# Placing eight gate projections between the last attention heads' scores, with separate buffers for those heads' second exponentials

## The chip, the cores and the metric

The kernel runs on one core of a Trainium2 chip. The metric is device time in microseconds (us) from the start to the end of one execution; the kernel before has a median of 1245.56 us over three runs (1245.56, 1245.99 and 1245.56). The engines are named as the profile names them: PE is TensorE (matrix products), PEld its weight loads, DVE is VectorE, ACT is ScalarE, POOL is GpSimd, SP is the engine that issues most DMAs.

## The reference

A decoder trunk of two layers over 512 tokens with 1024 features, all in float32. Layer 0 mixes with a causal convolution module, layer 1 with differential attention; behind each stand a SwiGLU feed-forward network and a gated per-layer input. The change lies in layer 1, in the attention and in one part of the gated input that is computed early:

```
# differential attention, 8 heads, for each head and each block of 128 queries
logits = q @ k.T + bias          # two components c = 0, 1 of 64 features each
logits = where(dist >= 0, logits, -inf)
probs  = softmax(logits)
w      = probs[c=0] - lam * probs[c=1]
o      = w @ v                    # 128 features per head
o      = rms_norm(o, sub_g) * (1 - lambda_init)
h      = h + concat(o) @ w_o
# ... feed-forward network ...
gate   = sigmoid(rms_norm(h, ple_norm_g) @ ple_w_gate)
h      = h + gate * (p[1] @ ple_w_proj)     # p[1] @ ple_w_proj needs nothing of h
```

## The kernel before, in words

The residual is kept transposed, as eight tiles `h0` to `h7` of 128 features by 512 tokens. A float32 product is made of three float32r matmuls, `mm3` (lines 165 to 169): each operand is split into a high and a low part, and low x high, high x high and high x low are accumulated in PSUM. "A product" below is one such group of three matmuls with 512 columns.

PSUM has four tiles for product sums and the heads' outputs (tag `mm`), two for scores (`sc`) and two for transposes (`tp`), lines 110 to 112.

The attention takes heads in pairs (heads 6 and 7 are pair 3). While the PE makes the projections to queries, keys and values (loop over `QKV`, lines 1291 to 1323), the heads that are ready run between the products as small stages:

- `stage_s(hd, qb)`, lines 1175 to 1208: the scores of one query block, for the components c = 0 and 1. Each is two matmuls (L1195, L1196) with n = 128, 256, 384 or 512 columns, for the block qb = 0 to 3. With n up to 256 both components share one `sc` tile, otherwise each takes its own. DVE then adds the bias and takes the extreme of each row (L1198), reading the `sc` tile and writing a buffer `e`; ACT makes the exponential in place in `e` (L1202); DVE makes the weights from both components (L1205 to L1207). For c = 0 the buffer comes from five rotating tiles, `big`. For c = 1 it is one of two single tiles: `acc` for even blocks, `rb` for odd ones, whatever the head (line 1197).
- `stage_t`, lines 1210 to 1218: up to four transposes on PE into a `tp` tile (L1215), and a copy by ACT to `wth` or `wtl` (L1217).
- `stage_a`, lines 1223 to 1251: the product with the values (L1228) into the head's `mm` tile; after blocks 1 and 3 DVE copies it to SBUF (L1236); after block 3 ACT squares the head's output (L1246) and POOL normalises it (L1247, L1248, L1251).
- `stage_o`, lines 1255 to 1261: four transposes of the head's output (L1258) and its split into high and low parts (ACT L205, DVE L206), which makes input k = hd of the output projection.
- `unit_end`, lines 1146 to 1168: the transposes (L1149) that make queries and keys of 128 tokens from a projection that ACT and POOL (L1143) have normalised, and their scaling and splits (ACT L1157 and L1158, POOL L1162, DVE L1165 and L1167).

The list `stages` (lines 1268 to 1272) holds all stages in order: for each step the scores of one block, `stage_a` of the block four before it and `stage_t` of the block two before it. The last blocks of heads 6 and 7 stand at the end of the order of blocks (lines 1265 to 1267).

27 of these stages are left when the last projection to queries and keys ends. They are run by `step()` (lines 1329 to 1339), which takes the next one from the list, and calls `stage_o` of a head when it is due. Steps are called from the loop over the eight gate projections, `p[1] @ ple_w_proj` (lines 1341 to 1346): each of these is two products (`project`, lines 369 to 376), so there are sixteen products, numbered P1 to P16 here. P1 to P8 take their weights from the tiles `B6` and `B7`, P9 to P16 from tiles that lie in `h0` to `h3`, whose residual was put aside in DRAM and is loaded back after them (`back`, lines 1285 to 1288). There is one step ahead of each projection and one after each product, 24 in all. The rest of the steps is called from the output projection (`linear`, lines 714 to 745, called at line 1364), whose first two output chunks m = 0 and 1 run together over k = 0 to 7.

Within these lists the order on each engine is set by a planner (`schedule_with_timeline_sim=True`, line 1508): the order in which the kernel is written gives the priority, and where an instruction is not yet ready by the planner's own clock, a later one that is ready goes first. Each engine then runs its own list strictly in that order. `tc.issue_after(x)` makes the instructions of a block come behind `x` on `x`'s engine; it is an order, not a wait.

Of the kernel before, what the change touches and what calls it, by code (L numbers as in the profile page):

```python
# [13 lines left out]
F32R = mybir.dt.float32r  # L14
# [6 lines left out]
P = 128  # L21
S = 512
D = 1024
NC = D // P
NH = 8
# [53 lines left out]
LA = 4  # L79
# [1 line left out]
OPS_AT = (1, 2, 4, 5)  # L81
HOOKS = {5: (None,), 6: (1, 3), 7: (0, 2, 4, 5)}
HT = S // 2
E1 = True
GLO = 1
QKV = (("q", 0, (0, 0, 0, 0)), ("v", 0, (1, 1, 1, 2)), ("q", 1, (1, 1, 1, 2)), ("q", 2, (1, 1, 2, 1)), ("v", 1, (1, 1, 2, 2)), ("q", 3, (1, 1, 1, 1)))

# [4 lines left out]
def trunk(ctx, tc, xT, xtok, pT, wts, diag, dww, vec, rel, onehot, lamv, out):  # L92
    nc = tc.nc
    V, A, G, T = nc.vector, nc.scalar, nc.gpsimd, nc.tensor
# [7 lines left out]
    def sb(shape, tag, bufs, dt=F32):  # L102
        uid[0] += 1
        return pool.tile(shape, dt, tag=tag, name=f"{tag}_{uid[0]}", bufs=bufs)
# [9 lines left out]
    big = lambda dt=F32, shape=(P, S): sb(list(shape), "big", 5, dt)  # L114
    f = lambda ap: ap.bitcast(F32)
# [6 lines left out]
    def col(name, i=0):  # L122
        a, _ = VEC[name]
        return vt[:, a + i : a + i + 1]

    ident = sb([P, P], "ident", 1)
# [7 lines left out]
    t = wk()[:, 0:P]  # L134
# [5 lines left out]
    t = tp()  # L140
# [7 lines left out]
    def weight(n=1024, pieces=1, between=(), eng=V, after=(None, None), home=None, parts=None, bufs=1):  # L148
        i = wnext[0]
        wnext[0] += 1  # L150
        raw = sb([P, 1024], *(home or ("wraw", 2)))
        hi = sb([P, 1024], *((parts[0], bufs) if parts else ("whi", 4)), F32R)
        lo = sb([P, 1024], *((parts[1], bufs) if parts else ("wlo", 4)), F32R)
        for k in range(pieces):
            cut = slice(k * n // pieces, (k + 1) * n // pieces)
            loaded[0] = nc.sync.dma_start(raw[:, cut], wts[i, :, cut])
            if k < len(between):
                between[k]()
            with tc.issue_after(after[1].ins) if after[1] else nullcontext():
                A.copy(hi[:, cut], raw[:, cut])  # L160
            with tc.issue_after(after[0].ins) if after[0] else nullcontext():
                eng.tensor_tensor(lo[:, cut], raw[:, cut], f(hi[:, cut]), ALU.subtract)  # L162
        return hi, lo

    def mm3(acc, a, b, first, last, **kw):
        (ah, al), (bh, bl) = a, b
        T.matmul(acc, al, bh, start=first, stop=False, **kw)  # L167
        T.matmul(acc, ah, bh, start=False, stop=False, **kw)  # L168
        return T.matmul(acc, ah, bl, start=False, stop=last, **kw)  # L169
# [15 lines left out]
    def wpart(w, k):  # L185
        return tuple(
            t[k // 4][:, (k % 4) * P : (k % 4 + 1) * P] if isinstance(t, list) else t[:, k * P : (k + 1) * P] for t in w
        )

    def both(t):  # L190
        return t[:, 0], t[:, 1]
# [97 lines left out]
    first = [tuple(sb([P, 1024], t, 4, F32R) for t in ("whi", "wlo")) for _ in range(4)]  # L289
# [69 lines left out]
    def pfeatures(layer, parts):  # L359
        for k, (hi, lo) in enumerate(parts):  # L360
            raw = sb([P, 1024], "wraw", 2)[:, :S]
            nc.sync.dma_start(raw, pT[layer, :, k * S : (k + 1) * S])
            A.copy(hi, raw)
            (G if layer == 0 else V).tensor_tensor(lo, raw, f(hi), ALU.subtract)
        return parts

    last_product = [None]

    def project(ph, m, w, o, step=lambda: None):

        acc = mm()
        for k in range(2):
            last_product[0] = mm3(acc, wpart(w, 2 * (m % 4) + k), ph[k], k == 0, k == 1)
            step()
        last_copy[0] = A.copy(o, acc)
        return o
# [11 lines left out]
    rb = None  # L388
# [161 lines left out]
    for c in range(NC):  # L550
        wa, wg = pairs[c]
        if c == 0:
# [6 lines left out]
            with tc.manual_schedule(engines={T.engine}):  # L559
# [5 lines left out]
                for k in range(NC):  # L565
                    late_rest(a1, pairs[1][0], k)
                    if k == 0:
                        rb = norm.rows()
# [4 lines left out]
        if c == 1:  # L573
            ph = pfeatures(0, [(sb([P, S], t, 2, F32R), sb([P, S], t, 2, F32R)) for t in ("wth", "wtl")])
# [36 lines left out]
    pp = []  # L611
    pw = [weight(), weight()]
# [450 lines left out]
    for k in range(2):  # L1063
        t = tp()
# [5 lines left out]
    def bias(hd):  # L1070
        b = sb([P, S], "bias", 2)
        nc.scalar.dma_start(b, bass.AP(scr.tensor, scr.offset + hd * RW, [[1, P], [1, S]]))
        return b
# [72 lines left out]
    def unit_end(pair, tb, q):  # L1146
        t = tp()
        for i in range(4):
            T.transpose(t[:, i * P : (i + 1) * P], q[:, i * P : (i + 1) * P], ident)  # L1149
        t4 = t.rearrange("p (h c t) -> p h c t", h=2, c=2)  # L1150
        cut = slice(tb * P, (tb + 1) * P)
        qs, ks, kl = qk[pair][0:2], qk[pair][2:4], qk[pair][4:6]

        qg, kg = col("q_g"), gains[:, 0:1]
        for c in range(2):
            own, other = HALVES[c], HALVES[1 - c]
            A.activation(qs[c][own, :, cut], t4[own, :, 0], AF.Copy, scale=qg[own])  # L1157
            A.activation(ks[c][own, :, cut], t4[own, :, 1], AF.Copy, scale=kg[own])  # L1158
            if KDUP == "A":
                A.activation(ks[c][other, :, cut], t4[own, :, 1], AF.Copy, scale=kg[own])  # L1160
            else:
                G.tensor_copy(ks[c][other, :, cut], f(ks[c][own, :, cut]))  # L1162
        for c in range(2):
            own, other = HALVES[c], HALVES[1 - c]
            V.scalar_tensor_tensor(  # L1165
                qs[c][other, :, cut], t4[own, :, 0], qg[own], f(qs[c][own, :, cut]), ALU.mult, ALU.subtract)
            V.scalar_tensor_tensor(  # L1167
                kl[c][own, :, cut], t4[own, :, 1], kg[own], f(ks[c][own, :, cut]), ALU.mult, ALU.subtract)

    last_block = [None, None]  # L1170
    biases = {}
    stats = {}
    state = {}

    def stage_s(hd, qb):
        if qb == 0:
            biases[hd] = bias(hd)
        b = biases[hd]
        n = (qb + 1) * P
        brev = bass.AP(b.tensor, b.offset + (S - 1) - (S - n), [list(b.ap[0]), [-1, n]])  # L1180
        qs, ks, kl = qk[hd // 2][0:2], qk[hd // 2][2:4], qk[hd // 2][4:6]
        i = hd % 2
        if qb == 0:
            stats[hd] = sb([P, 4, 6], "st", 2)
        es, st = [], stats[hd][:, qb]
        for c in range(2):
            cut = slice(qb * P, (qb + 1) * P)
            if not PACK or n > S // 2:
                acc = sc()
            elif c == 0:  # L1190
                both = sc()
                acc = both[:, : S // 2]
            else:
                acc = both[:, S // 2 :]
            T.matmul(acc[:, :n], qs[c][:, i, cut], ks[c][:, i, 0:n], start=True, stop=False)  # L1195
            T.matmul(acc[:, :n], qs[c][:, i, cut], kl[c][:, i, 0:n], start=False, stop=True)  # L1196
            e = sb([P, S], ("acc", "rb")[qb % 2], 1) if c and E1 else big()
            V.tensor_tensor_reduce(  # L1198
                out=e[:, :n], in0=acc[:, :n], in1=brev, scale=-1.0, scalar=3.0e38,
                op0=ALU.add, op1=ALU.min, accum_out=st[:, c : c + 1],  # L1200
            )
            A.activation(e[:, :n], e[:, :n], AF.Exp, scale=-1.0, bias=st[:, c : c + 1], accum_out=st[:, 2 + c : 3 + c])  # L1202
            es.append(e)

        V.reciprocal(st[:, 4:5], st[:, 3:4])  # L1205
        V.scalar_tensor_tensor(st[:, 5:6], st[:, 4:5], mlam, st[:, 2:3], ALU.mult, ALU.mult)
        last_block[0] = V.scalar_tensor_tensor(es[0][:, :n], es[1][:, :n], st[:, 5:6], es[0][:, :n], ALU.mult, ALU.add)  # L1207
        state[hd, qb] = es[0]
# [46 lines left out]
    def stage_o(hd):  # L1255
        t = tp()
        for i in range(4):
            T.transpose(t[:, i * P : (i + 1) * P], osb[hd][:, i * P : (i + 1) * P], ident)  # L1258
        hi, lo = both(sb([P, 2, S], f"A{hd}", 1, F32R))
        split_scaled(t, gains[:, 1:2], hi, lo)  # L1260
        ot[hd] = (hi, lo)
# [3 lines left out]
    todo = [(hd, qb) for hd in range(NH) for qb in range(4)]  # L1265
    todo.append(todo.pop(todo.index((NH - 2, 3))))
    todo.append(todo.pop(todo.index((NH - 1, 3))))
    stages = []
# [22 lines left out]
    for what, at, pace in QKV:  # L1291
        ws = slab(GLO if at > 0 else 0)
        for tb in range(4):
# [10 lines left out]
            if (what, at, tb) == ("q", 0, 1):  # L1304
                ph = pfeatures(1, [both(sb([P, 2, S], t, 1, F32R)) for t in ("B4", "B5")])
            elif (what, at, tb) == ("q", 0, 2):
                n = wnext[0]
                wnext[0] = PROJ1
                pw = [weight(parts=("B6", "B7"))]
# [17 lines left out]
    done, steps = [0], [0]  # L1327

    def step():

        steps[0] += 1
        if stages:
            n, s = stages.pop(0)
            s()
        else:
            n = 99
        while done[0] < NH and n >= todo.index((done[0], 3)) + LA + 4 and steps[0] > 4 * done[0] + 3:
            stage_o(done[0])
            done[0] += 1

    pp = []
    for m in range(NC):
        if m % 2 == 0:
            o2 = sb([P, 2, S], f"C{m // 2 + 2}", 2)
        step()
        pp.append(project(ph, m, pw[m // 4], o2[:, m % 2], step))

    def heads_until(k):
        while done[0] <= k:
# [13 lines left out]
    order = {m: last_block for m in (2, 3, 4, 5)}  # L1363
# [149 lines left out]
```

## Time and profile before

| | |
|---|---|
| median of the runs | 1245.56 us |
| the profiled execution | 1243.71 us |
| its span, first to last instruction | 1241.9 us |
| PE busy | 1230.2 us, 7048 matmuls |
| DVE, ACT, POOL busy | 878.7, 624.8, 464.9 us |
| the attention's scores L1195 | 627.4 to 790.9 us |
| the sixteen products of the gate projections | 766.9 to 793.7 us |

Times in the trace are us from the start of the span. A line of the timeline gives the start, the duration, the engine, the line of the kernel, the operation, the tile written and those read, the shape, and in brackets how long the engine was idle just before and what ended that. A matmul's duration is a modelled one and overlaps the next; the distance from one start to the next is what it costs. A line of the windows gives, for a stretch, the busy time of each engine with the number of its instructions, then the granted clock of PE (1.00 is full), the busy share of the DMA engines and GB/s.

### The profile page before, as it was taken

What the parts mean: (1) busy time and instruction counts of PE and PEld (TensorE: products, weight loads), DVE (VectorE), ACT (ScalarE), POOL (GpSimd) and SP (SyncE); (2) the same over time, 40 slices, a digit from 0 to 9 for tenths busy, and PEclk for the clock granted to TensorE, in tenths of its full rate; (3) what the DMA queues carried; (4) which work ended last, traced back from release to release, by engine and by line L of the source; (5) the groups of instructions that cost most, each with busy time, mean ns of one, the idle gap of its engine ahead of it and who ended that gap; (6) DMA issues with size and microseconds to landing.
All of it is one profiled execution on the core that took longest, in us unless ns stands there. A gap on an engine that the chain in (4) does not pass through costs nothing.

```text
span 1241.9 us, 18364 instructions
## 1 busy us (share of the span) xinstructions
PE 1230.2 (99%) x7048; PEld 1077.1 (87%) x7048; DVE 878.7 (71%) x1244; ACT 624.8 (50%) x1098; POOL 464.9 (37%) x351
## 2 busy tenths in 40 slices
PE   9999999999999999999999999999999999999998
PEld 7888788888998899888788888788889998999887
DVE  5999765975895479547677876647966885588535
ACT  7743454533553255435566877735434552455432
POOL 0953422024570454142436635041026640562220
PEclk9999999999999999999999999999999999999999
DMA  9655323233333332334432331142233333233331
GB/s 329 227 179 179 93 69 118 89 106 112 101 90 119 100 96 75 102 107 151 139 111 63 109 98 30 52 151 87 89 126 91 103 115 109 83 103 88 104 97 68
DMA packets 50020, 138.44 MB, mean 111 GB/s; under 512 B 5732, under 2 KB 10852, under 8 KB 49933
## 3 DMA queue, kind: packets, MB, share of 16 engines
q1 hardware_dynamic: 47664, 133.71, 34.2%
q10 hardware_dynamic: 2268, 3.57, 1.0%
q8 instruction: 55, 0.90, 0.3%
q14 instruction: 33, 0.26, 0.1%
HBM read 130.94 MB, written 6.31 MB: 111 GB/s over the span
## 4 chain that ended last, share of the span: by engine, by line
PE 84%; DVE 7%; DMA 3%; issue 3%; ACT 2%; POOL 2%; SPq 0%; ACTq 0%; DVEq 0%; POOLq 0%
PE mm L167 26%; PE mm L168 26%; PE mm L169 26%; DVE sc L508 2%; POOL wk L496 2%; DMA wraw<-in_wts 1%; DVE wlo L162 1%; PE mm L1228 1%; DMA B<-po 1%; PE sc L1195 1%; PE sc L1196 1%; PE tp L1215 1%; PE tp L1149 1%; DMA po<-big 0%; DVE wlo L822 0%
## 5 line engine op out<-in xcount | busy, mean ns | idle before, releaser
L160 ACT CAST whi<-wraw 128x1024 fp32r<-128x1024 f32 (+1 forms) x139 | 141.0, 1024 | 220.0 <-PE mm L169 106.8
L162 DVE TENSOR_TENSOR wlo<-wraw,whi 128x1024 fp32r<-128x1024 f32 (+1 forms) x135 | 174.2, 1296 | 82.5 <-ACT whi L160 81.8
L167 PE MATMUL mm<-A,wlo 128*128 128x512 f32 (+1 forms) x546 | 212.1, 388 | 0.1
L168 PE MATMUL mm<-A,whi 128*128 128x512 f32 (+1 forms) x546 | 211.1, 387 | 0.0
L169 PE MATMUL mm<-A,whi 128*128 128x512 f32 (+1 forms) x546 | 208.9, 387 | 0.1
L167 PE MATMUL mm<-B,wlo 128*128 128x512 f32 x352 | 137.0, 389 | 0.0
L168 PE MATMUL mm<-B,whi 128*128 128x512 f32 x352 | 137.0, 389 | 0.0
L169 PE MATMUL mm<-B,whi 128*128 128x512 f32 x352 | 135.6, 389 | 0.0
L228 POOL TENSOR_TENSOR acc<-acc,wk 128x512 f32<-128x512 f32 x35 | 60.3, 1724 | 191.6 <-ACT wk L227 190.9
L168 PE MATMUL mm<-C,whi 128*128 128x256 f32 x448 | 126.8, 283 | 0.0
L169 PE MATMUL mm<-C,whi 128*128 128x256 f32 x448 | 126.8, 283 | 0.0
L167 PE MATMUL mm<-C,wlo 128*128 128x256 f32 x448 | 126.8, 283 | 0.0
L167 PEld LDWEIGHTS mm<-A,wlo 128*128 128x128 f32 x546 | 102.7, 188 | 21.6 <-DVE h L1359 0.5
L169 PEld LDWEIGHTS mm<-A,whi 128*128 128x128 f32 x546 | 102.6, 188 | 21.5 <-DVE A L206 0.8
L168 PEld LDWEIGHTS mm<-A,whi 128*128 128x128 f32 x546 | 102.7, 188 | 20.3
L822 DVE TENSOR_TENSOR wlo<-A,whi 128x1024 fp32r<-128x1024 f32 x60 | 104.9, 1758 | 20.4 <-ACT whi L821 20.4
L821 ACT CAST whi<-A 128x1024 fp32r<-128x1024 f32 x60 | 62.9, 1048 | 55.0 <-PE mm L169 43.9
L831 POOL TENSOR_TENSOR A<-wraw 128x512 f32<-128x512 f32 x16 | 24.0, 1500 | 168.4 <-DMA wraw<-in_wts 143.3
L831 POOL TENSOR_TENSOR A<-A 128x512 f32<-128x512 f32 x16 | 25.1, 1566 | 163.6 <-DMA A<-in_wts 160.9
L167 PEld LDWEIGHTS mm<-C,wlo 128*128 128x128 f32 x448 | 86.0, 192 | 0.2
L168 PEld LDWEIGHTS mm<-C,whi 128*128 128x128 f32 x448 | 86.0, 192 | 0.2
L169 PEld LDWEIGHTS mm<-C,whi 128*128 128x128 f32 x448 | 86.0, 192 | 0.0
(332 smaller groups left out, 3065.3 us busy)
## 6 DMA issues: line engine op xcount, KB each, us to landing
wraw<-in_wts SPq DMA_DIRECT2D x159, 512.0 KB, 3.6
A<-in_wts SPq DMA_DIRECT2D x32, 512.0 KB, 3.6
wraw<-in_wts SPq DMA_DIRECT2D x16, 384.0 KB, 3.1
D<-in_diag SPq DMA_DIRECT2D x22, 256.0 KB, 4.8
C<-in_diag SPq DMA_DIRECT2D x16, 256.0 KB, 5.0
h<-in_xT SPq DMA_DIRECT2D x8, 256.0 KB, 3.9
B<-in_xtok SPq DMA_DIRECT2D x4, 512.0 KB, 7.7
rest<-h SPq DMA_DIRECT2D x8, 256.0 KB, 2.7
```

Source lines behind the costliest of these rows:

```text
L160: A.copy(hi[:, cut], raw[:, cut])
L162: eng.tensor_tensor(lo[:, cut], raw[:, cut], f(hi[:, cut]), ALU.subtract)
L167: T.matmul(acc, al, bh, start=first, stop=False, **kw)
L168: T.matmul(acc, ah, bh, start=False, stop=False, **kw)
L169: return T.matmul(acc, ah, bl, start=False, stop=last, **kw)
L228: self.last = self.eng.tensor_tensor(self.acc, self.acc, sq, ALU.add)
L496: G.tensor_tensor(pacc, pacc, pr, ALU.add)
L508: last_v_tap[0] = V.scalar_tensor_tensor(sum_, tap(j), wt(c, j), sum_, ALU.mult, ALU.add)
L821: A.copy(hi, src)
L822: V.tensor_tensor(lo, src, f(hi), ALU.subtract)
L831: G.tensor_tensor(s[:, 0], r1[:, 0], r1[:, 1], ALU.add)
L1149: T.transpose(t[:, i * P : (i + 1) * P], q[:, i * P : (i + 1) * P], ident)
```

## The change

The change makes three things.

Buffers: the second exponentials (c = 1) of heads 6 and 7 no longer go to `acc` and `rb`. Head 6 gets a tile of two halves under the tag `C0`, head 7 one under `C1`; the half is chosen by the parity of the block. These tags have two slots each; the slot that is taken held the queries of pair 2.

Order of the stages: the first eleven of the 27 left stages come in an order written out by hand.

Pace: a table says which steps follow each product, instead of one step after each. The letter `s` is a step, `S` a step whose PE instructions are put behind the product just made. There is one step ahead of P1, and 18 in the loop, so 19 instead of 24 before the output projection. P7 and P8 come behind the last `unit_end`'s transposes, and each product from P10 on comes behind the last score written so far. `stage_o` falls due a few steps later for heads 0 to 2 (at steps 7, 10 and 13, instead of 4, 8 and 12).

So on PE the written order is: scores (6,1), P1, P2, then P3 to P9, scores (6,2), P10, scores (7,0), P11, scores (7,1), P12, P13, transposes of (6,0), P14, scores (7,2), P15, scores (6,3), P16, scores (7,3), with the other stages between them; (6,2) is head 6, block 2.

```diff
-E1 = True
+PACE1 = ("","s","ss","","","","","","","S","S","Ss","","Sss","sSss","sss","s")
...
-    def project(ph, m, w, o, step=lambda: None):
+    def project(ph, m, w, o, step=lambda: None, gate=nullcontext):
         acc = mm()
         for k in range(2):
-            last_product[0] = mm3(acc, wpart(w, 2 * (m % 4) + k), ph[k], k == 0, k == 1)
+            with gate():
+                last_product[0] = mm3(acc, wpart(w, 2 * (m % 4) + k), ph[k], k == 0, k == 1)
             step()
...
     def unit_end(pair, tb, q):
-            T.transpose(t[:, i * P : (i + 1) * P], q[:, i * P : (i + 1) * P], ident)
+            turned[0] = T.transpose(t[:, i * P : (i + 1) * P], q[:, i * P : (i + 1) * P], ident)
...
     def stage_s(hd, qb):
-            T.matmul(acc[:, :n], qs[c][:, i, cut], ks[c][:, i, 0:n], start=True, stop=False)
+            first = T.matmul(acc[:, :n], qs[c][:, i, cut], ks[c][:, i, 0:n], start=True, stop=False)
+            if c == 0 or n > S // 2:
+                last_score[0] = first
             T.matmul(acc[:, :n], qs[c][:, i, cut], kl[c][:, i, 0:n], start=False, stop=True)
-            e = sb([P, S], ("acc", "rb")[qb % 2], 1) if c and E1 else big()
+            if c and hd >= NH - 2:
+                k = 2 * (hd % 2) + qb % 2
+                if k // 2 not in late_e:
+                    late_e[k // 2] = sb([P, 2, S], f"C{k // 2}", 2, F32R)
+                e = f(late_e[k // 2])[:, k % 2]
+            elif c:
+                e = sb([P, S], ("acc", "rb")[qb % 2], 1)
+            else:
+                e = big()
...
-        while done[0] < NH and n >= todo.index((done[0], 3)) + LA + 4 and steps[0] > 4 * done[0] + 3:
+        while done[0] < NH and n >= todo.index((done[0], 3)) + LA + 4 and steps[0] > max(4 * done[0] + 3, 3 * done[0] + 6):
...
+    order = [(stage_s, 6, 1), (stage_a, 5, 1), (stage_t, 5, 3), (stage_a, 5, 2), (stage_s, 6, 2),
+             (stage_s, 7, 0), (stage_s, 7, 1), (stage_a, 5, 3), (stage_t, 6, 0), (stage_a, 6, 0), (stage_t, 6, 1)]
+    rank = {at: i for i, at in enumerate(order)}
+    stages.sort(key=lambda s: rank.get((s[1].func, *s[1].args), len(order)))
+    products = [0]
+
+    def spaced():
+        products[0] += 1
+        for kind in PACE1[products[0]]:
+            with tc.issue_after(last_product[0].ins) if kind == "S" else nullcontext():
+                step()
+
+    def gate():
+        return tc.issue_after(last_score[0].ins) if products[0] > 8 else nullcontext()
+
+    step()
     for m in range(NC):
         if m % 2 == 0:
             o2 = sb([P, 2, S], f"C{m // 2 + 2}", 2)
-        step()
-        pp.append(project(ph, m, pw[m // 4], o2[:, m % 2], step))
+        with tc.issue_after(turned[0].ins) if m == 3 else nullcontext():
+            pp.append(project(ph, m, pw[m // 4], o2[:, m % 2], spaced, gate))
```

More of the change, by code (lines that the diff above doesn't have):

```diff
@@ L1170, in trunk @@
     last_block = [None, None]
+    late_e = {}
+    turned = [None]
+    last_score = [None]
     biases = {}
```

## The prediction, made before the changed kernel had run

> **What bounds the kernel now.** I read the page first, then the windows around the sixteen products, then the timelines of PEld, PE, DVE, ACT and POOL there.
>
> ```profile
> span 1241.9 us, 18364 instructions
> ...
> PE 1230.2 (99%) x7048; PEld 1077.1 (87%) x7048; DVE 878.7 (71%) x1244; ACT 624.8 (50%) x1098; POOL 464.9 (37%) x351
> ...
> PEclk9999999999999999999999999999999999999999
> ...
> PE 84%; DVE 7%; DMA 3%; issue 3%; ACT 2%; POOL 2%; SPq 0%; ACTq 0%; DVEq 0%; POOLq 0%
> ```
>
> PE is busy 99% of the span at full clock, and 84% of the chain that ended last is PE. So the change can win only time in which PE stands still, and 1241.9 - 1230.2 = 11.7 us of that exist in the whole kernel. The windows say how much lies where the change works:
>
> ```profile
> 766.00:776.00 10.00, 10.00 (x59) 8.47 (x58) 5.63 (x18) 7.12 (x20) 4.78 (x7) 1.00 0.01 2
> 776.00:783.00 7.00, 5.11 (x35) 4.16 (x34) 6.61 (x25) 6.66 (x23) 1.64 (x4) 1.00 0.01 2
> 783.00:787.00 4.00, 4.00 (x21) 3.26 (x19) 2.50 (x9) 2.47 (x7) 1.40 (x2) 1.00 0.18 42
> 787.00:792.00 5.00, 5.00 (x35) 4.29 (x34) 4.15 (x12) 4.61 (x16) 0.00 (x0) 1.00 0.20 71
> 792.00:807.00 15.00, 15.00 (x93) 12.97 (x91) 7.33 (x17) 9.30 (x23) 0.00 (x0) 1.00 0.22 71
> 822.00:850.00 28.00, 28.00 (x123) 23.18 (x124) 18.79 (x21) 15.06 (x22) 12.31 (x7) 1.00 0.37 108
> ```
>
> The columns after the length are PE, PEld, DVE, ACT and POOL. Only from 776 to 783 does PE stand (5.11 of 7.00); there DVE (6.61) and ACT (6.66) are nearly full. Right behind, from 783 to 787, it is the other way round: PE is full and DVE and ACT have 1.5 us free each. This is the clump that the change takes apart:
>
> ```profile
> 774.72 0.60 PE L1149 MATMUL tp<-ident,big 128*128 128x128 f32 x4
> ...
> 782.63 0.48 PE L167 MATMUL mm<-B,h 128*128 128x512 f32 x1
> 782.94 0.39 PE L168 MATMUL mm<-B,h 128*128 128x512 f32 x1
> 783.17 0.40 PE L169 MATMUL mm<-B,h 128*128 128x512 f32 x1
> ...
> 786.59 0.39 PE L169 MATMUL mm<-B,h 128*128 128x512 f32 x1
> ...
> 792.09 0.48 PE L167 MATMUL mm<-B,h 128*128 128x512 f32 x1
> ```
>
> P9 to P14 run as eighteen matmuls without a break from 782.63 to 786.59; P15 and P16 start at 792.09. A matmul of 512 columns costs 783.17 - 782.94 = 0.23 us, a product 0.69.
>
> **The waits that are to go.** [...]
>
> ```profile
> 776.44 0.19 PEld L1195 LDWEIGHTS sc<-C,C 128*128 128x128 f32 x1 [0.16 <-DVE st L1198]
> ...
> 777.26 0.19 PEld L1195 LDWEIGHTS sc<-C,C 128*128 128x128 f32 x1 [0.52 <-DVE st L1198]
> ...
> 778.49 0.42 PEld L1258 LDWEIGHTS tp<-ident,D 128*128 128x128 f32 x4 [0.69 <-ACT wtl L1217]
> ...
> 780.14 0.19 PEld L1195 LDWEIGHTS sc<-C,C 128*128 128x128 f32 x1 [0.23 <-DVE st L1198]
> ...
> 781.60 0.19 PEld L1195 LDWEIGHTS sc<-C,C 128*128 128x128 f32 x1 [1.16 <-DVE st L1198]
> ```
>
> The sum is 0.16 + 0.52 + 0.69 + 0.23 + 1.16 = 2.76 us. Four of the five wait for DVE to read a score out of one of the two `sc` tiles, one for ACT's copy out of a `tp` tile.
>
> [...]
>
> **Part by part.**
>
> *Pace and gates.* One product (0.69) now stands by order between each two of the scores (6,2), (7,0), (7,1), (7,2), (6,3), (7,3), two behind (7,1). Six products make 4.1 us of cover where 2.76 us are waited. The first, second and fourth wait (0.16, 0.52, 0.23) are each shorter than a product: gone. The fifth (1.16) is longer than P14 alone, but the buffers shorten it, next part. The third (0.69) belongs to `stage_o` of an early head, which now falls due later, with P12 and P13 near it; ACT must still get through its copies, so this wait may return: bounds 0 and 0.69. I take 0.15 as left over of all five.
>
> *The buffers.* These are the DVE rows that hold the fifth wait:
>
> ```profile
> 773.39 0.48 DVE L1165 SCALAR_TENSOR_TENSOR C<-tp,vec,C 64x256 fp32r<-64x256 f32 x1 [2.73 <-ACT C L1158]
> ...
> 780.25 0.48 DVE L1207 SCALAR_TENSOR_TENSOR big<-rb,st,big 128x256 f32<-128x256 f32 x1
> ...
> 781.12 0.41 DVE L1198 CUSTOM_DVE_ANT_0 rb<-sc,bias 128x256 f32<-128x256 f32 x1
> ...
> 781.46 0.61 DVE L1207 SCALAR_TENSOR_TENSOR big<-acc,st,big 128x384 f32<-128x384 f32 x1
> 781.99 0.74 DVE L206 SCALAR_TENSOR_TENSOR A<-tp,mhalf,A 128x512 fp32r<-128x512 f32 x1
> 782.65 0.28 DVE L1198 CUSTOM_DVE_ANT_0 acc<-sc,bias 128x128 f32<-128x128 f32 x1
> ...
> 787.60 0.56 DVE L1198 CUSTOM_DVE_ANT_0 acc<-sc,bias 128x384 f32<-128x384 f32 x1 [2.06 <-PE sc L1196]
> ```
>
> The second component of (7,1) can go into `rb` at 781.12 only once (6,1) is read out of it (780.25 to 780.73); that of (7,0) waits for (6,2) to leave `acc` (781.46) and is read at 782.65. Each holds an `sc` tile meanwhile. With a tile per head neither pair shares a buffer. This wins what is left of the fifth wait, nothing beyond. Where the later blocks' chain becomes shorter (`rb` is shared by (6,3) and (7,3) too) it costs and wins nothing, because PE is full from 792 to 807 anyway.
>
> *Breaks.* The first long matmul behind short ones costs 782.94 - 782.63 = 0.31 instead of 0.23: its weights, 0.19 in the PEld rows, can't load under a short predecessor. So a product by itself costs 0.08 more. Between 0 and 7 breaks are new (0 to 0.56 us); I take three, 0.25, since products behind scores of 384 and 512 columns, and P13 behind P12, have a long predecessor.
>
> *P7 and P8 behind the last `unit_end`.* It takes two products, 1.38 us, from the cover ahead of the transposes at 774.72. Were these late, PE would stand up to 1.38 us. They are not:
>
> ```profile
> 770.69 1.04 POOL L1143 TENSOR_TENSOR big<-big,r 128x512 f32<-128x512 f32 x1
> ```
>
> ```profile
> 773.01 0.48 PE L167 MATMUL mm<-B,B 128*128 128x512 f32 x1
> ```
>
> The input is ready at 771.73, and PE is in other work until 773.01, where P7 starts now. The edit costs nothing, and the splits behind these transposes start earlier, towards DVE's idle 2.73 us that end at 773.39.
>
> *The end.* P15 and P16 (1.38 us) now run ahead of the last score instead of behind it, and the last eight stages come from the output projection, behind its first products. So the cover of the last chain shrinks. Its rows:
>
> ```profile
> 796.07 0.75 DVE L1207 SCALAR_TENSOR_TENSOR big<-rb,st,big 128x512 f32<-128x512 f32 x1
> ...
> 805.72 2.36 DVE L162 TENSOR_TENSOR wlo<-wraw,whi 128x1024 fp32r<-128x1024 f32 x2 [0.30 <-ACT whi L160]
> ```
>
> ```profile
> 803.46 0.60 PE L1215 MATMUL tp<-ident,big 128*128 128x128 f32 x4
> ...
> 807.09 0.47 PE L167 MATMUL mm<-A,wlo 128*128 128x512 f32 x1
> ...
> 815.81 0.60 PE L1258 MATMUL tp<-ident,D 128*128 128x128 f32 x4
> ```
>
> ```profile
> 811.67 2.07 POOL L1251 TENSOR_TENSOR D<-D,r 128x512 f32<-128x512 f32 x1
> ```
>
> The weights of (7,3) are ready at 796.82 and transposed only at 803.46: 6.6 us of slack, more than 1.38. The head's normalisation ends at 813.74, PE asks for it at 815.81: 2.07 us of slack. If the planner puts the last transposes behind all products that cover them, the 3.63 us from 803.46 to 807.09 (copy, weight split, first product) would lose their two products, 1.38 us. I take 0.
>
> *Queues.* The moved scores of (7,0) issue one DMA, head 7's bias, on ACT's queue:
>
> ```profile
> 760.51 0.33 ACTq L1072 DMA_DIRECT2D bias<-scr  x1
> ```
>
> It goes some 16 us before DVE reads it. The loads of `h0` to `h3` on SP start when P9 to P16 are done; those end no later than before.
>
> **The sum.** 2.76 - 0.15 - 0.25 = 2.36 us. Against the profiled execution: 1243.71 - 2.36 = 1241.35, with a span near 1239.5. The median of the runs lies 1.85 us above that execution; moved by as much, it becomes 1245.56 - 2.36 = 1243.2. With the bounds (waits left 0 to 1.2, which is the second and third; breaks 0 to 0.56) the gain is 1.0 to 2.76, so 1242.8 to 1244.6. A measurement of this kernel tells about 0.2% from no change, 2.5 us, so this forecast lies at that edge.
>
> **The rivals.**
>
> *ACT is the bound of the stretch.* Its work from 776 to 792 is 6.66 + 2.47 + 4.61 = 13.74 us; at the share that it reaches under load, 6.66 / 7.00 = 95%, this takes 14.4 of the 16 us. So no more than 1.6 us could be won before the last scores, 1.3 after the breaks: 1244.3. For it speaks the third wait; against it, that PE can go on with the output projection while ACT catches up.
>
> *More than the idle rows.* With smoother DVE and ACT, some of the dozen breaks that already stand between 776 and 822 (0.08 each) go too, about 1 us: 2.36 + 0.9 = 3.3, 1242.3. Against it: PE takes as many turns between short and long matmuls as before.
>
> *The order turns against PE.* Before, PE's list held any ready product. Now P10 to P16 stand behind scores by order, and if a score waits for DVE, all of them wait. DVE has four splits of early heads (L206, 0.75 each) which the planner can put ahead of the reads that free `sc`. Then 4 x 0.75 = 3.0 us come on top of the 2.76 that stay: 1245.56 + 3.0 = 1248.6. It decides where DVE's work between two scores outlasts the product there, 0.69. For it: DVE is at 6.61 of 7.00 from 776 to 783. Against it: from 783 to 792 DVE works 6.65 of 9.00 and PE never stands.
>
> *The planner places as before.* Its own clock, not the chip, decided the clump; but `S` and the gates are orders it has to keep, so this is unlikely: 1245.6.
>
> **How the numbers follow.** Forecast 0.56, ACT bound 0.14, more than the rows 0.12, order against PE 0.14, no effect 0.04. Faster by over 0.2% needs 2.5 us: 0.24 of the forecast's 0.56 and all of the 0.12, together 0.36. Slower by over 0.2%: 0.10 of the 0.14 of the third. Within: 0.32 + 0.14 + 0.04 + 0.04 = 0.54. The range runs from the second rival's 1242.3, less 0.2, to 1245.9, which takes in the forecast, the ACT bound and no effect and leaves out the slower case: 1242.1 to 1245.9.
>
> **What would show it.** In the profile after, the PEld rows of the scores (6,2) to (7,3) should have no wait above 0.3 us on L1198, matmuls of one product each between them, the second components written to `C` and not to `acc` or `rb`, and DVE's idle 2.06 us at 785.5 gone. PE's busy time should stay near 1230 and the span fall by 2.4. I am wrong if a wait of PE above 0.5 us stands between 774 and 793, or a new one at the first products of m = 2 or at the last heads' L1258 between 800 and 822.

## The result and the profile after

The changed kernel takes 1241.3 us (median of six runs, 1240.72 to 1242.19), the kernel before in the same comparison 1245.57 (six runs, 1244.4 to 1247.1). The ratio is 0.9971, its 95% interval 0.9961 to 0.9981. So the change is faster, by 0.29% (0.19 to 0.39%), and the time lies 0.8 us below the low end of the predicted range.

The page of the changed kernel, whose profiled execution took 1242.19 us, has in its span, its busy times and its chain of work:

```profile
span 1240.4 us, 18361 instructions
...
PE 1229.5 (99%) x7048; PEld 1077.3 (87%) x7048; DVE 879.7 (71%) x1244; ACT 624.5 (50%) x1098; POOL 463.4 (37%) x351
...
PE 88%; DVE 5%; issue 3%; DMA 2%; ACT 1%; POOL 0%; SPq 0%; ACTq 0%; DVEq 0%; POOLq 0%
```

The matmuls are the same 7048, PE's share of the chain rose from 84% to 88%, and DVE's fell from 7% to 5%. The span of these two executions fell by only 1.5 us, less than the 4.27 us between the medians. The windows, in the same stretches as before, say where PE's idle time went:

```profile
766.00:776.00 10.00, 10.00 (x57) 8.62 (x56) 5.63 (x16) 7.78 (x22) 5.74 (x9) 1.00 0.01 2
776.00:783.00 7.00, 7.00 (x43) 6.18 (x42) 6.63 (x23) 6.10 (x19) 1.82 (x3) 1.00 0.11 20
783.00:787.00 4.00, 4.00 (x26) 3.60 (x25) 3.37 (x15) 3.49 (x13) 1.06 (x2) 1.00 0.27 100
787.00:792.00 5.00, 5.00 (x33) 4.35 (x32) 4.58 (x14) 4.62 (x16) 0.00 (x0) 1.00 0.23 67
792.00:807.00 15.00, 15.00 (x94) 12.91 (x93) 8.33 (x15) 9.15 (x26) 2.09 (x3) 1.00 0.26 75
```

From 776 to 783 PE is now full (7.00 for 5.11) and runs 43 matmuls for 35, while DVE is as busy as ever: 6.63 us, before 6.61. DVE was not made faster; PE has other work while it waits for DVE. The weight loads of the scores now have no wait at all, and one wait is left in the whole part from 766 to 806, in PEld:

```profile
804.52 0.19 PEld L167 LDWEIGHTS mm<-A,wlo 128*128 128x128 f32 x1 [0.26 <-PE mm L1242]
```

(The new lines shift the numbers: a score is L1199 and L1202 for L1195 and L1196, DVE's read of it L1212 for L1198, `stage_t` L1229 for L1215, `stage_a` L1242 for L1228, `stage_o` L1272 for L1258.) In PE's timeline P10, P11, P15 and P16 now stand singly among the scores; P12 to P14 run from 780.84 to 783.0, ahead of the second components of (7,0) and (7,1):

```profile
767.56 0.39 PE L167 MATMUL mm<-B,B 128*128 128x512 f32 x1
...
777.60 0.39 PE L167 MATMUL mm<-B,h 128*128 128x512 f32 x1
...
779.14 0.33 PE L1199 MATMUL sc<-C,C 128*128 128x128 f32 x1
...
779.42 0.45 PE L167 MATMUL mm<-B,h 128*128 128x512 f32 x1
...
782.24 0.27 PE L1229 MATMUL tp<-ident,big 128*128 128x128 f32 x1
782.27 0.47 PE L167 MATMUL mm<-B,h 128*128 128x512 f32 x1
782.58 0.39 PE L168 MATMUL mm<-B,h 128*128 128x512 f32 x1
...
800.92 0.60 PE L1229 MATMUL tp<-ident,big 128*128 128x128 f32 x4
...
803.17 1.06 PE L1242 MATMUL mm<-B,wtl 128*128 128x128 f32 x8
803.98 0.48 PE L169 MATMUL mm<-A,B 128*128 128x512 f32 x1
804.55 0.47 PE L167 MATMUL mm<-A,wlo 128*128 128x512 f32 x1
```

The second exponentials go to `C`, and DVE's idle 2.06 us are gone:

```profile
783.42 0.29 DVE L1212 CUSTOM_DVE_ANT_0 C<-sc,bias 128x128 f32<-128x128 f32 x1 [0.32 <-PE sc L1202]
```

**A measure that holds from run to run.** PE's matmuls are the same 4260, in the same order, up to P1, and the same again from the first product of the output chunk m = 2 on (for three kernels further below this second half does not hold). Between these two starts lies all that the change touches; this distance is called the window below. Its two ends after are the rows at 767.56 and 804.55: 36.99 us. Before, P1 starts at

```profile
766.94 0.39 PE L167 MATMUL mm<-B,B 128*128 128x512 f32 x1
```

and m = 2 at 807.09 (shown in the prediction): 40.15 us. The window became 3.16 us shorter. In the profiled execution after, P1 began 0.62 us later and the part behind the window (span less its end) took 1240.4 - 804.55 = 435.85 us, before 1241.9 - 807.09 = 434.81, so 1.04 more, with the same instructions. 3.16 - 0.62 - 1.04 = 1.50 us, which is the fall of the span. Whether the change makes those 1.66 us, or the runs do, is the first question for the experiments.

### The profile page after: what moved, and what is told of

The parts are those of the page before. It is cut to its first block, busy times and chain, and to the rows that moved or that the text cites. A ratio compares the mean times of both kernels' runs of the same rounds, so it can differ in the third digit from the quotient of the medians.

```text
span 1240.4 us, 18361 instructions
## 1 busy us (share of the span) xinstructions
PE 1229.5 (99%) x7048; PEld 1077.3 (87%) x7048; DVE 879.7 (71%) x1244; ACT 624.5 (50%) x1098; POOL 463.4 (37%) x351
## 4 chain that ended last, share of the span: by engine, by line
PE 88%; DVE 5%; issue 3%; DMA 2%; ACT 1%; POOL 0%; SPq 0%; ACTq 0%; DVEq 0%; POOLq 0%
PE mm L167 27%; PE mm L169 26%; PE mm L168 26%; PE sc L458 2%; DVE wlo L823 2%; PE mm L1242 1%; DMA wraw<-in_wts 1%; PE sc L1202 1%; PE sc L1199 1%; PE tp L1229 1%; DVE B L914 1%; PE tp L1150 1%; DMA po<-big 1%; DVE wk L906 0%; DVE sc L509 0%
```

## The experiments

In the tables and texts, "last score" is the start of the second component of (7,3), counted from P1. Before it is 24.0 us, after 24.2.

**Is it the window, or something outside it?** Theory A: the products' placing acts in the window alone and the rest is chance between runs. Theory B: part of the gain (or a loss) lies outside. Theory C: the buffers are what takes the waits away, the products' placing is beside the point. Four kernels ran side by side, then two more on another chip.

`again` and `again2` are the changed kernel, unaltered; `null` is the kernel before, unaltered.

> The changed kernel once more, unaltered, to separate the change from what differs from run to run. In the two traces PE needs 40.15 us from P1 to the first product of m = 2 before and 36.99 after, 3.16 less; the medians differ by 4.3. Theory A (the change acts in this window alone, and the rest is chance in DMA waits elsewhere): the window is again 37.0 +- 0.1, the difference of the medians falls to 3.2 +- 0.7. Theory B (something outside the window is faster as well, such as the loads of h0 to h3 or the output projection's weights): the medians differ by 4 or more again and a stretch outside the window is shorter in this trace as well.

> The changed kernel a third time, on the same chip as the kernel before run as a candidate. Theory A: window 36.99 +- 0.1; median 3.2 +- 0.8 below that of before. Theory B: 4 or more below.

> The kernel before, unaltered, timed against itself, with a profile of its own. Theory A (the window alone changes, the rest of the difference is chance): the window from P1 to the first product of m = 2 is 40.15 +- 0.1 again, the median lies within 1 us of the other runs of before, and the start of P1 and the rest behind the window differ from the first profile by up to 2 us each with identical instructions. Theory B (the change wins outside the window too): P1 starts later or the rest behind the window is longer than in the changed kernel's profiles, 764.7 to 767.6 and 434.8 to 435.9.

| kernel | its median (runs) | kernel before beside it | ratio, 95% interval |
|---|---|---|---|
| again | 1240.09 (5) | 1244.13 (23) | 0.9965, 0.9952 to 0.9977 |
| again2 | 1241.02 (11) | 1243.83 (23) | 0.9976, 0.9967 to 0.9984 |
| null | 1244.53 (12) | 1243.83 (23) | 1.0002, 0.9993 to 1.0011 |

The ends of the window in `again`, `again2` and `null`, from PE's timelines:

```profile
764.72 0.39 PE L167 MATMUL mm<-B,B 128*128 128x512 f32 x1
...
801.70 0.47 PE L167 MATMUL mm<-A,wlo 128*128 128x512 f32 x1
```

```profile
768.22 0.39 PE L167 MATMUL mm<-B,B 128*128 128x512 f32 x1
...
805.19 0.47 PE L167 MATMUL mm<-A,wlo 128*128 128x512 f32 x1
```

```profile
766.00 0.39 PE L167 MATMUL mm<-B,B 128*128 128x512 f32 x1
...
806.12 0.47 PE L167 MATMUL mm<-A,wlo 128*128 128x512 f32 x1
```

The windows are 36.98, 36.97 and 40.12 us: each kernel's window repeats within 0.03 us. Outside it the times scatter: P1 starts at 764.72 and at 768.22 in two executions of one program, and the kernel before starts it at 766.94 and 766.00. `again` by itself met what had been written down for B: 4.04 us between the medians, and P1 2.2 us earlier than before. `again2` and `null` speak against it: 2.81 us between the medians, and P1 of `again2` comes later than in either trace of the kernel before. So A stands and B falls. Over all runs the changed kernel has a median of 1241.13 us (22 runs, 1238.31 to 1242.19), the kernel before 1244.26 (66 runs with those of `null`, 1241.84 to 1247.1); the difference, 3.13, agrees with the window's 3.16.

**Which of the parts does it?** `buffers` is the kernel before with the new buffers alone:

```diff
-            e = sb([P, S], ("acc", "rb")[qb % 2], 1) if c and E1 else big()
+            if c and hd >= NH - 2:
...
+                e = f(late_e[k // 2])[:, k % 2]
```

> The kernel before with the separate buffers for heads 6 and 7 alone; order, pace and gates as before. Theory A (the placing of the products removes the waits, the buffers only shorten the fifth): the clump P9 to P14 stays, the first four waits (1.6 us) stay, of the fifth (1.16) some 0.5 to 1.1 goes; gain 0.5 to 1.1 us. Rival C (the sc tiles held by acc and rb are the cause of the waits, the placing does nothing): waits of the scores on L1198 fall below 0.3 each and the gain is 2 to 3 us.

1244.16 us (11 runs) against 1244.13, ratio 1.0001 (0.9992 to 1.0009); window 39.82 us, 0.33 less than before, so less than the 0.5 to 1.1 that theory A gave it too. The two small waits of 0.17 at the last score, shown further below, are gone. The fifth wait moves on by one score:

```profile
780.30 0.34 PE L1196 MATMUL sc<-C,C 128*128 128x384 f32 x1
...
781.56 0.19 PEld L1196 LDWEIGHTS sc<-C,C 128*128 128x128 f32 x1 [1.06 <-DVE st L1207]
```

```profile
781.08 0.41 DVE L1207 CUSTOM_DVE_ANT_0 C<-sc,bias 128x256 f32<-128x256 f32 x1
```

The first component of (7,2), which waited 1.16 before, runs at 780.30 without a wait: with a buffer of its own (7,0) leaves its `sc` tile earlier. But the second component of (7,2) then waits 1.06 for the other tile. DVE reads (7,1) out of that at 781.08, 14.3 us behind P1 (before, at 781.12, 14.2), without idle time ahead of it: there it is DVE's list that holds the tile, and not a shared buffer.

`pace` is the changed kernel with the old buffers:

```diff
-            if c and hd >= NH - 2:
...
-            else:
-                e = big()
+            e = sb([P, S], ("acc", "rb")[qb % 2], 1) if c else big()
```

> The changed kernel with acc and rb for the second exponentials of heads 6 and 7 again; order, pace and gates stay. Theory A: gain 2 to 2.7 us, with a wait of up to 0.5 us at a score of (7,1) or (7,2). Rival C: the waits come back, gain under 1 us, since P10 to P16 now stand behind scores that acc and rb hold up.

1241.58 us (10 runs), ratio 0.9978 (0.9969 to 0.9987), window 36.96. No wait at a score came back, where up to 0.5 us had been expected. So the buffers bring nothing in the changed kernel, and C falls.

`no_orders` keeps the table but not the orders on PE: a step marked `S` is a plain step, and products no longer come behind the last score.

```diff
-            with tc.issue_after(last_product[0].ins) if kind == "S" else nullcontext():
+            with tc.issue_after(last_product[0].ins) if False else nullcontext():
...
-        return tc.issue_after(last_score[0].ins) if products[0] > 8 else nullcontext()
+        return tc.issue_after(last_score[0].ins) if False else nullcontext()
```

> The changed kernel without the orders S and without the gates from P10 on: list, number of steps, due steps of stage_o, the order behind the last unit_end and the buffers stay. The planner is free again to pull products forward, and in the written order four of them (P9 to P12) go ahead of (6,2) in one clump. Theory A: two or three of the waits come back behind the clump, gain 0.5 to 1.8 us. Rival C (buffers) and rival D (the list of stages and the later stage_o remove the waits, the orders are an ornament): gain 3 us as with the orders.

1241.56 us (8 runs), ratio 0.9974 (0.9963 to 0.9984), window 37.09. P9 to P12 now run in one clump ahead of (6,2), the last score comes only at 27.4 us, and still PEld has a single wait in the window:

```profile
805.65 0.19 PEld L167 LDWEIGHTS mm<-A,wlo 128*128 128x128 f32 x1 [0.26 <-PE mm L1242]
```

This was a surprise: the orders that my prediction built on, one product between each two scores, are not needed either.

**The list, the due steps or the number of steps?** What is left is the order of the stages by hand, the later `stage_o`, and the table's plain numbers: fewer steps ahead of P9 to P16. Theory D: the list, or the later `stage_o`, takes the waits away. Theory E: the pace does, as the last heads' scores then meet products that are still to be made. Two kernels take one part out of the changed kernel (`old_due` has the old condition for `stage_o`, `no_list` lacks the sort), two put one part into the kernel before (`list_only` has the list alone; `bare_pace` the numbers of the table as plain steps, one step ahead of the loop, and nothing else):

```diff
+    PACE1 = ("", "s", "ss", "", "", "", "", "", "", "s", "s", "ss", "", "sss", "ssss", "sss", "s")
...
+    step()
     for m in range(NC):
...
-        step()
-        pp.append(project(ph, m, pw[m // 4], o2[:, m % 2], step))
+        pp.append(project(ph, m, pw[m // 4], o2[:, m % 2], spaced))
```

> The changed kernel, but stage_o of heads 0 to 2 falls due at steps 4, 8 and 12 again. The window from P1 to the first product of m = 2 was 40.15 before and 36.99, 36.99, 36.96 and 37.09 in four kernels with pace and list, so one profile tells. Theory E (it is the pace, fewer steps ahead of P9 to P16, that lets the planner take products where scores are not yet freed): window 37.0 to 37.3. Theory D (the third wait, 0.69, was that of an early stage_o; the list and the later due steps remove the waits): 37.6 to 38.5, with a wait of PE at L1258's counterpart behind ACT.

> The changed kernel without the hand-written order of eleven stages: they come in the list's old order, with the same pace, orders and due steps. Theory E: window 37.0 to 37.3. Theory D: some waits come back, 37.8 to 39.

> The kernel before with nothing but the hand-written order of the eleven stages; 24 steps, one after each product and one ahead of each projection, old due steps and buffers. Theory E: the waits stay, 39.3 to 40.5. Theory D: 37.0 to 38.5.

> The kernel before with nothing but the pace: 19 steps behind the products as in the changed kernel's table, no orders, no list, old due steps, old buffers. Theory E: window 37.0 to 37.5, nearly all of the change's 3.16. Theory D: 38.5 to 40, as the list and the due steps are missing.

| kernel | window, us | last score, us | one run, us (before beside it: 1245.08) |
|---|---|---|---|
| old_due | 37.03 | 26.8 | 1240.22 |
| no_list | 37.01 | 27.4 | 1241.92 |
| list_only | 40.47 | 29.3 | 1244.98 |
| bare_pace | 41.07 | 30.2 | 1246.79 |

D falls: each of its parts can be left out (`pace_orders`, below, has neither), and the list alone wins nothing. Its waits only move; the three longest of seven in PEld are:

```profile
776.08 0.42 PEld L1215 LDWEIGHTS tp<-ident,big 128*128 128x128 f32 x4 [0.90 <-PE sc L1196]
...
777.79 0.42 PEld L1258 LDWEIGHTS tp<-ident,D 128*128 128x128 f32 x4 [0.53 <-ACT wtl L1217]
...
781.67 0.30 PEld L1228 LDWEIGHTS mm<-B,wth 128*128 128x128 f32 x2 [0.76 <-ACT wth L1217]
```

E holds in its first half only. The bare pace removes the waits at the scores (of before's 3.27 us one of 0.48 is left), and yet its window is the longest of all. The loss has another place, as PEld shows:

```profile
783.38 0.42 PEld L1258 LDWEIGHTS tp<-ident,D 128*128 128x128 f32 x4 [0.48 <-ACT wth L1217]
...
804.36 0.97 PEld L1228 LDWEIGHTS mm<-B,wtl 128*128 128x128 f32 x8 [0.66 <-ACT wtl L1217]
...
808.06 0.48 PEld L1258 LDWEIGHTS tp<-ident,D 128*128 128x128 f32 x4 [2.74 <-POOL D L1251]
```

The way there is read in PE's timeline of the same kernel:

```profile
791.73 0.48 PE L167 MATMUL mm<-A,h 128*128 128x512 f32 x1
...
797.77 0.48 PE L1195 MATMUL sc<-C,C 128*128 128x512 f32 x1
...
803.07 0.60 PE L1215 MATMUL tp<-ident,big 128*128 128x128 f32 x4
...
808.07 0.89 PE L1258 MATMUL tp<-ident,D 128*128 128x128 f32 x4 [2.55 <-POOL D L1251]
808.60 0.77 PE L167 MATMUL mm<-A,wlo 128*128 128x512 f32 x1
```

The planner takes products of the output projection (`mm<-A,h`, from 791.73 on) ahead of the last scores, the second component of (7,3) starts only at 797.77, 30.2 us behind P1, and its weights are transposed at 803.07. By then the products of m = 0 and 1, which should cover the chain of the last two heads (copy by ACT, product with the values, normalisation on POOL), are used up: PE waits 0.66 for ACT's copy and 2.74 for the transposes of head 6, which the row puts down to POOL. The sum, 0.48 + 0.66 + 2.74 = 3.88 us, is more than before's 3.27.

POOL is not alone in this. PE's list has head 6's transposes (808.07) ahead of the first product of m = 2 (808.60), while in the kernel before and in every kernel with a window near 37 they stand 6.9 us behind it. And the weights of m = 2 are late as well, by DVE's row

```profile
805.90 3.19 DVE L162 TENSOR_TENSOR wlo<-wraw,whi 128x1024 fp32r<-128x1024 f32 x2
```

of which one took 1.23 us by itself at 811.79, so that, as an estimate from this, the first ended near 807.1. With the products of m = 2 ahead of the transposes PE would still have stood until then, some 1.8 of the 2.74 us. What is late is the whole end of the last heads, and not one engine.

**What saves the end?** Theory E2: any one other part of the change, beside the pace, holds the last scores early enough. Its rival is G of the expectations. Four kernels add one part each to the bare pace: `pace_orders` the orders `S` and the products behind the last score, `pace_list` the list, `pace_due` the later `stage_o`, `pace_buffers` the buffers. The last three differ from `bare_pace` by the lines shown in the change; `pace_orders` is the changed kernel without buffers, list, later `stage_o`, and the order behind `unit_end`.

```diff
+        while done[0] < NH and n >= todo.index((done[0], 3)) + LA + 4 and steps[0] > max(4 * done[0] + 3, 3 * done[0] + 6):
```

is all that `pace_due` adds to `bare_pace`.

> Pace and the orders S and the gates from P10 on; no list, old due steps, old buffers. Theory E2 (the pace removes the waits at the scores, and any one of the other parts keeps the planner from leaving the last scores and transposes late, which cost 2.74 + 0.66 us of new waits with the pace alone): window 37.0 to 37.3. Theory F (two parts together are needed for the end): the scores' waits stay away, a wait of 1 to 3 us stays between 800 and 809, window 38 to 41.

> Pace and the hand-written order of eleven stages; no orders, old due steps, old buffers. Theory E2: 37.0 to 37.3. Theory F: 38 to 41, with the wait at the last heads' L1258 or at L1228.

> Pace and the later due steps of stage_o for heads 0 to 2; no orders, no list, old buffers. Theory E2: 37.0 to 37.3. Theory F: 38 to 41; of the four this is the one that should matter least at the end, since it touches heads 0 to 2 alone.

> Pace and the separate buffers for heads 6 and 7; no orders, no list, old due steps. With the pace alone the second component of (7,3) was read at 798.88, behind the one of (6,3) leaving rb at 797.80, and the last transposes came at 803.07. Theory G (rb is what makes the end late there): the last scores come 1 to 2 us earlier, the wait at L1258 falls below 1 us, window 37 to 38.5. Theory F: 39 to 41, as the planner's order of the last stages stays.

| kernel | window, us | last score, us | one run, us (before beside it: 1244.32) |
|---|---|---|---|
| pace_orders | 37.26 | 24.5 | 1242.83 |
| pace_list | 40.69 | 31.3 | 1243.67 |
| pace_due | 37.11 | 27.3 | 1244.10 |
| pace_buffers | 40.97 | 30.2 | 1246.62 |

(By one run alone `pace_due` would look like no gain; its window tells otherwise. P1 started only at 769.49 us there, 2.55 later than before, outside of what it changes.) E2 holds for the orders (where one wait of 0.49 is left at a score) and for the due steps, not for list and buffers. G falls with `pace_buffers`, whose last score comes no earlier than without the buffers, and F, that two parts are needed, falls with the first two. The due steps, which I had taken to matter least, are enough: PEld of `pace_due` has in the window two waits left,

```profile
790.27 0.42 PEld L1258 LDWEIGHTS tp<-ident,D 128*128 128x128 f32 x4 [0.28 <-PE sc L1196]
...
806.57 0.19 PEld L167 LDWEIGHTS mm<-A,wlo 128*128 128x128 f32 x1 [0.26 <-PE mm L1228]
```

while `pace_list` waits in PEld at the end where `bare_pace` does, and in PE for the weights of m = 2:

```profile
803.88 0.97 PEld L1228 LDWEIGHTS mm<-B,wtl 128*128 128x128 f32 x8 [0.64 <-ACT wtl L1217]
805.56 0.42 PEld L1258 LDWEIGHTS tp<-ident,D 128*128 128x128 f32 x4 [0.72 <-POOL D L1251]
806.70 0.19 PEld L167 LDWEIGHTS mm<-A,wlo 128*128 128x128 f32 x1 [0.72 <-PE tp L1258]
```

```profile
806.73 0.47 PE L167 MATMUL mm<-A,wlo 128*128 128x512 f32 x1 [0.51 <-DVE wlo L162]
```

It also has three waits between 782 and 784 (0.32 at a score, 0.43 and 0.61), so the pace does not keep the stretch of the scores free of waits in every order.

The last score sorts all kernels with the pace: at 24 to 27.4 us the window is 36.96 to 37.26, at 30 and more it is 40.69 to 41.07. That a due step shifts the last score by 2.9 us (30.2 to 27.3) is measured; by which choices of the planner was not followed. The three long windows are the kernels whose PE list has head 6's transposes ahead of m = 2, so these windows hold four matmuls more, 232 for 228. Counted from P1 over 300 matmuls, which are the same ones in all kernels, it is 56.1 us before, 52.9 to 53.2 in the good ones, and 57.8, 56.2 and 57.9 in `bare_pace`, `pace_list` and `pace_buffers`: the sorting stays, but `pace_list` is no worse than the kernel before.

No kernel beats the changed one: all good ones lie at about 37.0, where PE has next to no wait to give. Not tried: the orders, or the later `stage_o`, with the old, even pace. So it is shown that pace and due steps together are enough, and pace and orders; that the pace is needed is not shown.

## Why the prediction was right or wrong

The direction and the place were right: idle time of PE at the last heads' scores is filled with products, and 1241.3 is faster than before. Of its means two turned out not to be needed: the separate buffers, and the order of one product between two scores.

The step that failed is the sum, 2.76 - 0.15 - 0.25 = 2.36 us. All three terms were mis-sized (the rows held 3.27 us and not 2.76; 0.15 was charged for waits left at the scores, where none is; breaks cost about nothing and not 0.25), and the runs showed 3.16 in its place. A fourth term, the scatter of the runs, stood at next to nothing (0.2 us) without a reason. With 3.16 alone the forecast would have been 1245.56 - 3.16 = 1242.4, inside the range. That the six runs came out another 1.1 us lower is chance, as all runs together show 3.13 between the medians. The terms one by one:

*The waits, 2.76 us.* All five are gone, as said. But I counted five of eight. Three more, of 0.17 each, stand in PEld before the change, and I had passed over them because each is small:

```profile
775.52 0.42 PEld L1215 LDWEIGHTS tp<-ident,big 128*128 128x128 f32 x4 [0.17 <-PE sc L1195]
...
790.94 0.19 PEld L1195 LDWEIGHTS sc<-C,C 128*128 128x128 f32 x1 [0.17 <-DVE st L1198]
791.40 0.47 PEld L1258 LDWEIGHTS tp<-ident,D 128*128 128x128 f32 x4 [0.17 <-ACT wth L1217]
```

With them before has 2.76 + 0.51 = 3.27, after 0.26: 3.01 us of the window's 3.16. The other 0.15 I can't put down to one row. PEld's rows are also a little distorted: between short matmuls loads overlap (the two loads of the score at 776.44 and 776.54 start 0.10 us apart and last 0.19 each), so an idle time counted from the end of the load ahead can miss up to 0.09 there, by these rows.

*What is left of the waits, 0.15.* The third wait, which I thought might return on ACT, did not: 0. ACT's 6.66 us from 776 to 783 became 6.10.

*Breaks, 0.25.* This term failed by its reasoning. I read that a long matmul behind a short one takes 0.31 for 0.23 to its successor, and charged 0.08. I did not look at the step ahead of it. Before, the load of the product's first matmul, 782.60 to 782.79, does outlast the start of its matmul at 782.63, where the third one's, 782.95 to 783.14, ends ahead of its own at 783.17; but these rows don't show that it costs anything. After, the transpose at 782.24 has its successor at 782.27, 0.03 later, and the product's first matmul its own at 782.58, 0.31 later: 0.34 together. Eight short matmuls ahead of a long one take 803.98 - 803.17 = 0.81; if the last of them has 0.03 as well, the other seven have 0.11 each, and 0.11 + 0.23 = 0.34. So the break only moves the time from one row into the next, and its price is about nothing.

These three make 0.51 + 0.15 + 0.25 = 0.91 us, less the 0.26 that stays at 804.52, 0.65; 2.36 + 0.65 = 3.01. The window gained 3.16 - 2.36 = 0.80 us more than forecast, the 0.15 without a row among it.

*The level.* The forecast took 2.36 from the median of the three runs shown, 1245.56. Over 66 runs the kernel before has 1244.26, 1.3 less, and 1244.26 - 3.16 = 1241.10 is what 22 runs of the changed kernel show (1241.13). In the first comparison before stood at 1245.57 again, so its difference, 4.27, is larger by 1.1 than the window's and larger than the 4.04 and 2.81 of the two repetitions. My range reached no lower than 1242.1 because its low end was a rival's time, 1242.3, less 0.2; it held next to nothing for the runs, whose scatter (1238.31 to 1242.19 for one program) is as wide as the gain.

*The buffers.* I let them remove the rest of the fifth wait. Alone they let the score pass that waited 1.16, and the next one waits 1.06; in the changed kernel the products cover it, three in a row (P12 to P14), and `pace` shows that the buffers add nothing. That they win nothing beyond was right.

*P7 and P8 behind `unit_end`, the queues.* No wait came up at these places, as forecast.

*The end.* I took 0, with 1.38 us as the price if its cover were lost. For the change as a whole 0 was right: from the last transposes to m = 2 it takes 804.55 - 800.92 = 3.63 us, as before. But it is a balance: with the bare pace the cover is lost, and PE waits 0.66 + 2.74 us, more than I gave, since head 6's normalisation on POOL and the weights of m = 2 on DVE are late as well as the copy.

*The rivals.* ACT as the bound (1244.3), the order turned against PE (1248.6) and no effect (1245.6) are refuted by the windows: PE is full from 766 to 807. "More than the idle rows" (3.3 us, 1242.3) was the nearest in size, but not by its reason: the gain is in the idle rows, eight of them, and breaks have next to no price. And the words "one product between each two scores" describe the change, not its cause: `no_orders` gets 37.09 without that.

## What to carry to other kernels

Where an engine that bounds the kernel waits in a few places, sum the idle time of all its rows between two starts that both programs have, small rows too, and compare that window rather than the whole time; here it repeats within 0.03 us where whole runs of one program differ by 4 to 5. Spare work that is ready early should be spent where the waits are; how exactly it stands between them mattered little here, as kernels with the products in one clump (`no_orders`) or held back one by one (`pace_orders`) both end within 0.3 us of the changed one. What is held back for one place is taken from another: look at what covers the chain that comes last, at when its first link starts, and at what stands in the list ahead of the work that could cover it.

## What the runs showed of the hardware

In `bare_pace` the long wait of PE is followed by a lower granted clock. The windows around this wait, which ends with POOL, are (the clock is the last but two of the columns):

```profile
803.00:808.00 5.00, 2.29 (x15) 1.59 (x13) 2.84 (x5) 3.75 (x12) 3.16 (x4) 1.00 0.00 0
808.00:812.00 4.00, 3.94 (x13) 3.20 (x14) 2.05 (x3) 1.74 (x2) 3.20 (x4) 0.57 0.81 240
812.00:820.00 8.00, 8.00 (x39) 6.59 (x38) 2.99 (x3) 1.74 (x2) 0.00 (x0) 1.00 0.46 144
```

PE worked 2.29 of the 5 us up to 808, with 2.55 us of idle time in one piece, and from 808 to 812 the granted clock was 0.57, from 812 to 820 it was 1.00. PE's timeline there and at full clock again:

```profile
809.60 0.63 PE L169 MATMUL mm<-A,whi 128*128 128x512 f32 x1
810.03 0.63 PE L167 MATMUL mm<-A,wlo 128*128 128x512 f32 x1
...
812.23 0.40 PE L167 MATMUL mm<-A,wlo 128*128 128x512 f32 x1
812.46 0.39 PE L168 MATMUL mm<-A,whi 128*128 128x512 f32 x1
```

A long matmul takes 0.43 us there (810.03 - 809.60), 0.23 at full clock (812.46 - 812.23).

Two shorter waits of PE were not followed by a lower clock. Far ahead of the change, PE waits 1.26 us for a DMA in the kernel before (until 121.11) and 1.74 us in the changed one (until 121.81), and from 122 to 126 the granted clock is 1.00 in both. Whether the length of a wait decides is not shown by these three.

The other thing is how unequal executions of one program are: over the sixteen traces P1 starts anywhere from 764.72 to 769.49 us, with the same list of PE's instructions ahead of it. In the traces of before and after a part of it arises between 105 and 126 us, where PE's only wait ends with a DMA (of `in_diag`): 1.26 us before (P1 at 766.94), 1.74 after (767.56). Why these loads land at different times stays open.
